# A hybrid two-block network on one core: the state space preparation's parameter chain from VectorE to GpSimd, and its within-chunk products turned round

## The chip, the core and the metric

The kernel runs on one core of a Trainium2 chip. The core has TensorE (PE in the profile; its weight loads are PEld), VectorE (DVE), ScalarE (ACT), GpSimd (POOL) and SyncE (SP, which here only issues DMAs). The time is that of one execution on the device in microseconds, a median of several runs. Beside it there is the profile of one execution, whose span runs from the first to the last instruction.

## The reference, cut to what matters

Two blocks run one after the other on a sequence of 256 tokens of 1024 channels. The first has two layers of a mixer (gated linear attention, a short convolution and latent attention side by side) and of attention over a memory. The second has two layers: a feed-forward part, a mixer, a feed-forward part. The mixer of its first layer is the state space one, the place of the change:

```python
dt = jnp.exp(log_dt)[:, None]
mag = jnp.exp(a_re * dt)
ab_re = mag * jnp.cos(a_im * dt)
ab_im = mag * jnp.sin(a_im * dt)
den = a_re * a_re + a_im * a_im
z_re = ((ab_re - 1.0) * a_re + ab_im * a_im) / den
z_im = (ab_im * a_re - (ab_re - 1.0) * a_im) / den
bb_re = z_re[..., None] * b_re - z_im[..., None] * b_im
bb_im = z_re[..., None] * b_im + z_im[..., None] * b_re
...
# x_t = ab * x_(t-1) + bb u_t (complex), by an associative scan
y = (jnp.einsum('bsgp,ghp->bsgh', x_re, c_re) - jnp.einsum('bsgp,ghp->bsgh', x_im, c_im)
     + d_skip * ug)
```

There are 64 groups of 16 channels with 64 complex states each. None of the parameters depends on the tokens.

## The kernel before, in words

Time is cut into 64 chunks of 4 tokens, and the state space layer becomes a few matrix products with tables that depend on the parameters alone. `s5_prep` makes the tables in the background of the first block and of the second block's first feed-forward part, long before `s5` reads them.

`s5_prep` first loads the parameters to 128 partitions (two groups of 64 states) x 32 columns (pairs of groups). Then follows the chain of parameters, all in 128x32 instructions: the sine and cosine (`sin_reduced`, with ScalarE), the powers 0 to 4 of a in `pw`, the powers of its phase factor up to the 128th in `E`, and z in `zr` and `zi`. A complex product is `cmul`, six instructions through `TT` (L1136). The chain stands on VectorE; one reciprocal (L1183) is in the midst of it. Its end feeds six 128x512 instructions on GpSimd that make `bb`.

Then `s5_prep_tile` runs for tiles 0 to 7, of four pairs each. A tile's steps are, in order: the load of C; X on GpSimd (tiles `pX0`, `pX1`, through `pt`); transposes of C, copied by ScalarE to `pcb` (L1249, L1250); C times powers of a on GpSimd (`pt`, then `pv`); transposes of X, copied by ScalarE (L1272) and stored; the products within a chunk, `pcb` with X, into a bank `pq`, which ScalarE copies to `pt` (L1285) and VectorE completes and spreads (L1287, L1293); the turning frame on GpSimd (`pt` and `pv` with `E`); and the last store. Stores to the stash are DMAs of GpSimd's queue.

Three things set the order. GpSimd keeps the order of the program (`InOrder`, whose helper's line L60 all its instructions carry), the foreground's few GpSimd instructions among them: `rm` and `rg` in the first block, `rf` as the first of the second block. The instructions of the other engines, and the DMAs of SyncE, are put in an order when the program is built, by a model of their times; at run time each engine keeps that order. How far the background gets is decided in `bg`, which the foreground calls after each of its steps. It gives the background a credit, a share (0.4 in the first block, 0.7 in the feed-forward part) of the counted time of the foreground's products, and each step of the background is charged with GpSimd's counted time, but 1000 at least. `InOrder` counts 2.6 ns for each column of an instruction, 0.9 for a memset and 1000 for a DMA.

Weights come in chunks through two `raw` buffers: SyncE loads (L143), ScalarE makes `hi` (L155), VectorE makes `lo` (L156), and then the buffer is free. When all steps are done, `s5_inputs` reloads some of the preparation's tiles: `bb` and two `pv` take the first tables from the stash (L1336), `prm` and `E` take other constants (L1364). These loads stand in SyncE's queue among those of the weights.

Of the kernel before, what the change touches and what calls it, by code (L numbers as in the profile page):

```python
# [14 lines left out]
AF = mybir.ActivationFunctionType  # L15
# [16 lines left out]
def ov(ap, dims):  # L32
    """The same start and partitions as ap, with other free dimensions [step, count]."""
    return bass.AP(tensor=ap.tensor, offset=ap.offset, ap=[list(ap.ap[0])] + [list(d) for d in dims])
# [14 lines left out]
class InOrder:  # L49
    """GpSimd with its instructions issued in the order of the program; counts about the ns that they take."""  # L50
# [13 lines left out]
class Products:  # L64
    """TensorE; counts about the ns that its products take."""
# [13 lines left out]
class Net:  # L79
# [13 lines left out]
    def bg(self):  # L93
        """Steps of the work in the background, in step with the products."""
        self.owed = min(self.owed + self.share * (self.PE.ns - self.at), 10000)
        self.at = self.PE.ns
        while self.owed > 0:
            g = self.G.ns
            if next(self.side, 1):
                break  # L100
            self.owed -= max(self.G.ns - g, 1000)
        self.at = self.PE.ns

    def keep_clock(self, n, p, w, x):
        """Products to a bank that nothing reads before it is written anew, in a chain of small steps: TensorE's clock
        would be halved after 3.4 us with little to do."""
        for _ in range(n):
            self.PE.matmul(p[:w.shape[-1]], w, x, start=True, stop=True)
# [28 lines left out]
    def chunk(self, parts, a, b, p=P, engine=None, to=None, rush=False, pieces=None, n=0):  # L137
        """parts: (dram access [p, .., ..], slice of b) that fill [p, a, b].  With pieces (the part of raw [p, n], the
        part of [p, a, b]) the parts are of raw instead."""
# [9 lines left out]
        # a large one in two steps, between which more urgent work can go  # L149
# [9 lines left out]
    def wcols(self, W, c0, n, k0=0, nk=KD, parted=False, **kw):  # L159
        """Columns c0.. of W [K, N] with nk tiles of 128 rows from tile k0."""  # L160
# [4 lines left out]
    def mm3(self, out, w, x, start, stop, **kw):  # L165
        """out += w.T @ x, w and x pairs of parts."""
# [5 lines left out]
    def projT(self, p, ws, x, nk=KD):  # L172
        """p [cols, i, tokens] over nk tiles of rows; ws: for each i (hi, lo) [p, nk, cols]; x (hi, lo) [p, nk, S]."""
# [5 lines left out]
    def proj2(self, w, x, m=P, n=2, tag="ps"):  # L179
        """[m, n, S] from n times m columns of the chunk w."""  # L180
# [4 lines left out]
    def rows(self, W, c0, n, x, tag="ps", take=None):  # L185
        """[tokens, n] = x.T @ W[:, c0:c0 + n], a bank for each token tile."""
# [13 lines left out]
    def rows2(self, W, c0, x, tag="ps"):  # L200
        """[tokens, t, 256] = x.T @ W[:, c0:c0 + 256], both token tiles in one bank."""
# [10 lines left out]
    def out_proj(self, W, xs, nc_, evac):  # L212
        """For each two output tiles evac(pair, psum [P, 2, S]) of W.T @ x, xs a list of pairs of parts, one for each
        tile of 128 rows; nc_ columns in a chunk."""
# [26 lines left out]
    def setup(self):  # L241
# [28 lines left out]
        # the gain of the heads of 96, four times over, in rows of 128  # L270
# [9 lines left out]
    def gain_rows(self, w, parts, eng):  # L280
        """Gains to rows of a tile (those of fewer than 128 entries twice, 64 apart)."""
# [16 lines left out]
    def load_gains(self, w):  # L298
        """The rows to columns."""
# [22 lines left out]
    def nat_T(self, xn, between=None):  # L322
        """xn [p, 2, D] natural; for each pair of tiles psum [P, 2, S]"""
# [10 lines left out]
    def nat_stats(self, xn, tag):  # L334
        """The token factor of a norm from natural rows."""
# [7 lines left out]
    def sumsq(self, src, n, tag="ps", weights=None):  # L343
        """[tokens, 2] sums over the n tiles of src [p, n, S] of their squares; next to them, [tokens, 4], the sums of
        the squares times weights by column [p, n]."""
# [22 lines left out]
    def rpow(self, ms, n, w, tag, p=P, eps=EPS, to=None):  # L368
        """(ms / n + eps) ** -0.5, [p, w]"""
# [5 lines left out]
    def bcast(self, cols, dst, tag="ps"):  # L375
        """[P tokens, 2] -> [P, S], the same on each partition."""
# [9 lines left out]
    def xhat(self, src, g, dst=None):  # L386
        """(hi, lo) of src [p, 8, S] times a gain by row."""
# [9 lines left out]
    def norm(self, gkey, l, tag):  # L397
        """Parts of hT * gain, the token factor as columns and as [P, S]."""
# [16 lines left out]
    def sin_reduced(self, out, a, k, phase, sign):  # L415
        """out = sign * sin(a + phase); k = (a + phase) / 2 pi, overwritten, as is a."""
# [12 lines left out]
    def mixer(self, l):  # L429
# [22 lines left out]
        # the weights in the order of their use, each loaded ahead of the work on the one before  # L452
# [3 lines left out]
        def heads_of(c0):  # L456
            """Heads of 48 columns to 64 apart."""
# [4 lines left out]
        def queries():  # L462
            """Heads of 64 + 32 columns, and once more the last 32 with their halves swapped."""
# [19 lines left out]
        # latent projections; glr, kr and kr with its halves swapped  # L483
# [36 lines left out]
        # gated linear attention: decays  # L520
# [31 lines left out]
        # latents, gained; keys and values  # L552
# [46 lines left out]
        # latent attention  # L599
# [40 lines left out]
        # gated linear attention: within and between chunks of 64  # L640
# [64 lines left out]
        # gates and the short convolution  # L705
# [60 lines left out]
        # products with the gates  # L766
# [14 lines left out]
    def mem_in(self, l):  # L781
        """Parts of mem * gain."""
# [48 lines left out]
    def cross(self, l):  # L831
# [6 lines left out]
        def mem_v(i):  # L838
            """The memory's values for two heads."""
# [63 lines left out]
        # the first two heads' part of three banks ahead of the rest  # L903
# [76 lines left out]
    def final_norm(self):  # L980
        """hT = norm_final(hT) and the parts of the next norm's input; returns that norm's token factor."""
# [7 lines left out]
        # with m and m2 the means of hT^2 and (hT gf)^2, the two norms' factors are f = (m + eps)^-1/2 and, in all,  # L989
        # f (f^2 m2 + eps)^-1/2 = (m2 + eps (m + eps))^-1/2  # L990
# [14 lines left out]
    def xhat_part(self, gkey, l, m2):  # L1005
        """Two tiles of the parts of hT * gain."""
# [3 lines left out]
    def pre_norm(self, gkey, l, tag, ready=False):  # L1010
        """First the parts of hT * gain, then the token factor."""
# [5 lines left out]
    def ffn(self, name, l, pre=None, out=None, then=None, rb=None):  # L1017
        """hT += 0.5 * swiglu(norm(hT)); rb: the token factor as [P, S], where it is known"""
# [10 lines left out]
        for m2 in range(KF // 2):  # L1029
            v = []  # L1030
            for c0 in (0, D_FF):
                with self.behind(self.parted if m2 == 0 and c0 else ()):
                    w = self.wcols(WI, c0 + m2 * 256, 256)
                # the third waits for the token factor, without which the first two don't leave their banks
# [54 lines left out]
    def residual_rows(self):  # L1089
        """hT back to [tokens, D]"""  # L1090
# [10 lines left out]
    # Time runs in 64 chunks of 4.  A pair of groups (32 channels, 2 x 64 states) is one matrix product:  # L1101
    # rows (time in chunk, channel) or (group, state).  Between chunks the complex recurrence is a real
    # scan in a frame that turns with the phase of a^4.
# [3 lines left out]
    def s5_prep(self):  # L1107
# [28 lines left out]
        TT = lambda o, a, b, op: V.tensor_tensor(o, a, b, op=op)  # L1136
# [9 lines left out]
        # powers 0..4 of a, and its phase factor's powers  # L1146
        V.memset(pw[:, 0, 0, :], 1.0)
        V.memset(pw[:, 1, 0, :], 0.0)
        TT(pw[:, 0, 1, :], v["mag"], v["cos"], MUL)
        TT(pw[:, 1, 1, :], v["mag"], v["sin"], MUL)  # L1150

        def cmul(o, a, b, s, E=TT):
            E(o[0], a[0], b[0], MUL)
            E(s[0], a[1], b[1], MUL)
            E(o[1], a[0], b[1], MUL)
            E(s[1], a[1], b[0], MUL)
            E(o[0], o[0], s[0], SUB)
            E(o[1], o[1], s[1], ADD)
# [8 lines left out]
        # u^4, u^8, .., u^128: cos, -sin, sin  # L1167
        E = self.pz.tile([P, 6, 3, H], F32, name="E", tag="E", bufs=1)
        cmul((E[:, 0, 0], E[:, 0, 2]), u2, u2, tmp)
        for k in range(6):  # L1170
            if k:
                cmul((E[:, k, 0], E[:, k, 2]), *2 * ((E[:, k - 1, 0], E[:, k - 1, 2]),), tmp)
            V.tensor_scalar(E[:, k, 1], E[:, k, 2], -1.0, None, op0=MUL)
# [5 lines left out]
        # z = (a - 1) / a_ct  # L1179
# [832 lines left out]
```

## Time and profile before

| | us |
|---|---|
| median of 3 runs | 1525.09 |
| lowest and highest run | 1522.07 to 1529.53 |
| span of the profiled execution | 1519.9 |
| TensorE, VectorE, ScalarE, GpSimd busy in it | 1437.0, 1016.3, 739.8, 322.0 |

A row of the profile names a line of the kernel, the engine, the operation, and what is written from what (buffer numbers left out), with partitions x columns. In a row of the timeline the first number is the start in us from the span's start, the second the time from the first start to the last end of the instructions merged in it, xN their number; in brackets stands the engine's idle time before it and who ended that. An fp32 product shows as two records. The granted clock is TensorE's share of its full speed.

### The profile page before, as it was taken

What the parts mean: (1) busy time and instruction counts of PE and PEld (TensorE: products, weight loads), DVE (VectorE), ACT (ScalarE), POOL (GpSimd) and SP (SyncE); (2) the same over time, 40 slices, a digit from 0 to 9 for tenths busy, and PEclk for the clock granted to TensorE, in tenths of its full rate; (3) what the DMA queues carried; (4) which work ended last, traced back from release to release, by engine and by line L of the source; (5) the groups of instructions that cost most, each with busy time, mean ns of one, the idle gap of its engine ahead of it and who ended that gap; (6) DMA issues with size and microseconds to landing.
All of it is one profiled execution on the core that took longest, in us unless ns stands there. A gap on an engine that the chain in (4) does not pass through costs nothing.

```text
span 1519.9 us, 28406 instructions
## 1 busy us (share of the span) xinstructions
PE 1437.0 (95%) x11767; PEld 1346.7 (89%) x11767; DVE 1016.3 (67%) x1768; ACT 739.8 (49%) x1248; POOL 322.0 (21%) x434
## 2 busy tenths in 40 slices
PE   8999999899998988997879999999999989999999
PEld 7888998889998978996769999899999976899987
DVE  6896756777676766539947764566775478666754
ACT  6844566544554443431244444455444367554442
POOL 2053432442546872003200000010000031000000
PEclk9998999999999999998899999999999988999999
DMA  7553644544645655564775555655555622155554
GB/s 193 155 152 102 205 150 124 167 132 150 212 146 163 212 201 191 184 220 170 209 149 180 194 187 181 198 184 172 171 194 177 212 81 92 38 175 183 189 188 144
DMA packets 239868, 255.58 MB, mean 168 GB/s; under 512 B 27664, under 2 KB 221145, under 8 KB 238844
## 3 DMA queue, kind: packets, MB, share of 16 engines
q1 hardware_dynamic: 234060, 234.71, 48.7%
q0 software_dynamic: 5392, 18.99, 4.7%
q8 instruction: 92, 1.51, 0.4%
q14 instruction: 36, 0.29, 0.1%
q10 hardware_dynamic: 288, 0.07, 0.0%
HBM read 235.66 MB, written 18.09 MB: 167 GB/s over the span
## 4 chain that ended last, share of the span: by engine, by line
PE 65%; DVE 9%; issue 9%; DMA 7%; POOL 7%; ACT 3%; SPq 0%; POOLq 0%; ACTq 0%; DVEq 0%
PE ps L72 56%; PE pb L72 4%; DMA raw<-in_ffn_w_in_dram 3%; POOL pv L60 3%; DVE lo L156 3%; PE pq L72 2%; POOL pt L60 2%; PE po L72 2%; DMA raw<-in_w_in_dram 1%; PE pb L76 1%; ACT hi L155 1%; POOL pX L60 1%; DMA stash<-pv 1%; DMA memn<-in_mem_dram 1%; DVE ra L1458 1%
## 5 line engine op out<-in xcount | busy, mean ns | idle before, releaser
L156 DVE TENSOR_TENSOR lo<-raw,hi 128x1024 fp32r<-128x1024 f32 (+4 forms) x383 | 486.2, 1285 | 153.2 <-PE ps L72 82.8
L155 ACT ACTIVATE hi<-raw 128x1024 fp32r<-128x1024 f32 (+2 forms) x395 | 407.6, 1072 | 327.3 <-DMA raw<-in_ffn_w_in_dram 119.7
L72 PE MATMUL ps<-xh,hi 128*128 128x256 f32 x1848 | 526.0, 285 | 13.2 <-ACT hi L155 11.2
L72 PE MATMUL ps<-xh,lo 128*128 128x256 f32 x1848 | 523.1, 283 | 7.7 <-DVE lo L156 7.6
L72 PE MATMUL ps<-xl,hi 128*128 128x256 f32 x1848 | 522.6, 283 | 0.4 <-DVE xl L392 0.4
L72 PEld LDWEIGHTS ps<-xh,hi 128*128 128x128 f32 x1848 | 351.2, 190 | 19.4 <-ACT hi L155 13.0
L72 PEld LDWEIGHTS ps<-xh,lo 128*128 128x128 f32 x1848 | 351.1, 190 | 11.8 <-DVE lo L156 9.8
L72 PEld LDWEIGHTS ps<-xl,hi 128*128 128x128 f32 x1848 | 351.1, 190 | 5.0 <-issue 3.2
L72 PE MATMUL ps<-gl,hi 128*128 128x256 f32 x576 | 164.3, 286 | 0.4 <-DVE gl L1479 0.4
L72 PE MATMUL ps<-gh,lo 128*128 128x256 f32 x576 | 164.4, 286 | 0.0
L72 PE MATMUL ps<-gh,hi 128*128 128x256 f32 x576 | 163.6, 286 | 0.5 <-ACT gh L1478 0.4
L72 PEld LDWEIGHTS ps<-gl,hi 128*128 128x128 f32 x576 | 111.3, 193 | 1.3 <-DVE gl L1479 0.6
L72 PEld LDWEIGHTS ps<-gh,hi 128*128 128x128 f32 x576 | 110.3, 193 | 1.5 <-ACT gh L1478 0.9
L72 PEld LDWEIGHTS ps<-gh,lo 128*128 128x128 f32 x576 | 110.6, 192 | 0.5 <-issue 0.2
L1040 DVE TENSOR_TENSOR ab<-ps,rbf 128x512 f32<-128x512 f32 x66 | 45.4, 689 | 76.2 <-PE ps L72 69.4
L72 PE MATMUL ps<-L,hi 128*128 128x256 f32 (+1 forms) x384 | 72.3, 286 | 1.5 <-DVE e L549 1.4
L237 ACT ACTIVATE gh<-e 128x512 fp32r<-128x512 f32 x44 | 27.7, 630 | 91.8 <-DVE e L1047 91.8
L72 PEld LDWEIGHTS ps<-L,hi 128*128 128x128 f32 (+1 forms) x384 | 58.1, 182 | 2.5 <-DVE e L549 1.7
L72 PE MATMUL ps<-L,lo 128*128 128x256 f32 (+1 forms) x192 | 53.9, 282 | 0.0
L1045 ACT ACTIVATE e<-ab 128x512 f32<-128x512 f32 x44 | 27.7, 630 | 37.1 <-DVE ab L1040 37.0
L60 POOL TENSOR_TENSOR rkvs<-rkvsa,mhalf 128x2 f32<-128x2 f32 x1 | 1.6, 1607 | 191.0 <-DVE rkvsa L371 191.0
L1046 DVE SCALAR_TENSOR_TENSOR e<-e,ab 128x512 f32<-128x512 f32 x44 | 32.6, 740 | 8.5 <-ACT e L1045 8.3
(578 smaller groups left out, 2455.1 us busy)
## 6 DMA issues: line engine op xcount, KB each, us to landing
raw<-in_ffn_w_in_dram SPq DMA_DIRECT2D x88, 1024.0 KB, 5.1
raw<-in_ffn_w_out_dram SPq DMA_DIRECT2D x34, 1024.0 KB, 5.1
stash<-pv POOLq DMA_DIRECT2D x24, 512.0 KB, 3.8
raw<-in_w_in_dram SPq DMA_DIRECT2D x11, 1024.0 KB, 8.6
raw<-in_ffn_w_out_dram SPq DMA_DIRECT2D x12, 768.0 KB, 4.6
raw<-in_w_out_dram SPq DMA_DIRECT2D x8, 1024.0 KB, 5.2
raw<-in_w_in_dram SPq DMA_DIRECT2D x14, 512.0 KB, 5.6
rec<-stash SPq DMA_DIRECT2D x4, 1536.0 KB, 7.2
```

The lines of the kernel that those rows point to most:

```text
L60: return self.tc.keep_in_program_order(f(out, *a, **k))
L72: return self.engine.matmul(out, w, x, **k)
L76: return self.engine.transpose(out, x, ident)
L155: self.nc.scalar.activation(dst(hi), src(raw), AF.Copy)
L156: (engine or self.nc.vector).tensor_tensor(dst(lo), src(raw), dst(hi).bitcast(F32), op=SUB)
L237: self.nc.scalar.activation(hi, src, AF.Copy)
L1040: V.tensor_tensor(v[-1], p, rb2, op=MUL)
L1045: A.activation(th, v[0], AF.Tanh, scale=0.5)
L1046: V.scalar_tensor_tensor(th, th, 1.0, v[0], op0=ADD, op1=MUL)
L1458: V.tensor_tensor(a[:, c, :], a[:, c, :], b[:, 1 - c, :], op=SUB if c else ADD)
```

## The change

In `s5_prep` the chain's products, sums, scalar steps and two memsets are issued on GpSimd. The reciprocal, the copies and the sine and cosine stay where they were. In `s5_prep_tile` the products within a chunk swap their operands: the 32 columns of C are the weights and the 128 columns of X move; four such products write to four times 32 rows of one bank. The bank then holds the transpose of what is wanted, so ScalarE copies it to the second 128 columns of a `pt` tile and TensorE turns it into a further bank of `pq`. Comments and descriptions of functions fall away too; those lines are left out here.

```diff
-        TT = lambda o, a, b, op: V.tensor_tensor(o, a, b, op=op)
+        TT = lambda o, a, b, op: G.tensor_tensor(o, a, b, op=op)
...
-        V.memset(pw[:, 0, 0, :], 1.0)
-        V.memset(pw[:, 1, 0, :], 0.0)
+        G.memset(pw[:, 0, 0, :], 1.0)
+        G.memset(pw[:, 1, 0, :], 0.0)
...
-        def cmul(o, a, b, s, E=TT):
-            E(o[0], a[0], b[0], MUL)
...
+        def cmul(o, a, b, s):
+            TT(o[0], a[0], b[0], MUL)
...
-            V.tensor_scalar(E[:, k, 1], E[:, k, 2], -1.0, None, op0=MUL)
+            G.tensor_scalar(E[:, k, 1], E[:, k, 2], -1.0, None, op0=MUL)
...
         V.reciprocal(v["dt"], v["t0"])
-        V.tensor_scalar(v["th"], pw[:, 0, 1, :], -1.0, None, op0=ADD)
+        G.tensor_scalar(v["th"], pw[:, 0, 1, :], -1.0, None, op0=ADD)
...
-        pg = self.ps("pq")[:, :P].rearrange("p (q c) -> p q c", q=4)
-        for q in range(4):
-            for c in range(2):
-                PE.matmul(pg[:, q, :], X[c][:, q * P:(q + 1) * P], cb[:, c, q].rearrange("p g h -> p (g h)"),
-                          start=c == 0, stop=c == 1)
+        pw_ = self.ps("pq")
+        for c in range(2):
+            for q in range(4):
+                PE.matmul(pw_[32 * q:32 * q + 32, :P], cb[:, c, q].rearrange("p g h -> p (g h)"), X[c][:, q * P:(q + 1) * P],
+                          start=c == 0, stop=c == 1, skip_group_check=True)
+        gt = self.pt()
+        gm, gw = gt[:, :P], gt[:, P:2 * P]
+        A.activation(gw, pw_[:, :P], AF.Copy)
+        pg = self.ps("pq")[:, :P]
+        PE.transpose(pg, gw, self.ident)
+        pg = pg.rearrange("p (q c) -> p q c", q=4)
         last = rec()
         tz = last[:, :512]
-        gm = self.pt()[:, :P]
```

## Rows read from the trace of the kernel before

**Rows 1.** The page's busy times: us, share of the span, instructions.
```profile
PE 1437.0 (95%) x11767; PEld 1346.7 (89%) x11767; DVE 1016.3 (67%) x1768; ACT 739.8 (49%) x1248; POOL 322.0 (21%) x434
```

**Rows 2.** Windows: length, busy us (count) of PE PEld DVE ACT POOL, clock, DMA share, GB/s.
```profile
80.00:100.00 20.00, 19.81 (x152) 18.15 (x153) 19.99 (x79) 9.45 (x17) 6.19 (x5) 1.00 0.36 106
...
110.00:115.00 5.00, 0.43 (x4) 0.23 (x2) 5.00 (x9) 2.12 (x3) 4.73 (x6) 0.78 0.82 262
115.00:124.00 9.00, 8.57 (x31) 6.41 (x32) 5.52 (x10) 3.58 (x6) 6.74 (x7) 0.55 0.22 63
```

**Rows 3.** Timeline of TensorE, 109 to 119 us.
```profile
115.43 1.54 PE L72 MATMUL po<-asT,mv 128*64 128x256 f32 x4 [4.99 <-ACT asT L627]
```

**Rows 4.** Waits of SyncE's queue, 60 to 130 us: us in total, times, longest.
```profile
SPq L143 <- DVE lo L156: 50.9, 6, 13.9
```

**Rows 5.** Waits of SyncE's queue, 440 to 620 us; timeline of TensorE behind them.
```profile
SPq L1336 <- POOL pt L60: 14.0, 1, 14.0
...
560.05 0.58 PE L72 MATMUL ps<-xh,hi 128*128 128x256 f32 x1 [5.38 <-ACT hi L155]
```

**Rows 6.** Instructions of L1136, first and last of twelve rows: ns min/median/max, starts.
```profile
L1136 DVE TENSOR_TENSOR prm<-prm x19: 179/184/506, 55.4 to 94.6; 128x32 f32<-128x32 f32 x19
...
L1136 DVE TENSOR_TENSOR r<-r x1: 186/186/186, 60.8 to 60.8; 128x32 f32<-128x32 f32 x1
```

**Rows 7.** Timeline of VectorE, ten instructions of the chain between the two starts.
```profile
75.13 0.19 DVE L1136 TENSOR_TENSOR pw<-pw,prm 128x32 f32<-128x32 f32 x1
...
76.14 0.18 DVE L1136 TENSOR_TENSOR pw<-pw 128x32 f32<-128x32 f32 x1
```

**Rows 8.** GpSimd: timeline at 150 us; its groups by form (busy, mean ns).
```profile
150.45 0.24 POOL L60 TENSOR_TENSOR pt<-pv,E 128x32 f32<-128x32 f32 x1
...
151.30 0.29 POOL L60 TENSOR_TENSOR pt<-pv,E 128x64 f32<-128x64 f32 x1
...
L60 POOL TENSOR_TENSOR pv<-pv,E 128x32 f32<-128x32 f32 x8 | 4.6, 579 | 0.0
```

**Rows 9.** Timeline of VectorE, two of the same instruction.
```profile
93.48 1.21 DVE L156 TENSOR_TENSOR lo<-raw,hi 128x1024 fp32r<-128x1024 f32 x1
...
97.21 2.08 DVE L156 TENSOR_TENSOR lo<-raw,hi 128x1024 fp32r<-128x1024 f32 x1
```

**Rows 10.** Timeline of VectorE, then GpSimd: power chain, reciprocal, bb.
```profile
74.52 0.19 DVE L1136 TENSOR_TENSOR pw<-prm 128x32 f32<-128x32 f32 x1
...
90.73 0.34 DVE L1183 RECIPROCAL prm<-prm 128x32 f32<-128x32 f32 x1
...
92.45 1.07 POOL L60 TENSOR_TENSOR bb<-pX,prm 128x512 f32<-128x512 f32 x1 [29.61 <-DVE prm L1136]
```

**Rows 11.** Timeline of TensorE: tile 4's products and what follows.
```profile
440.43 1.87 PE L72 MATMUL pq<-pcb,pX 128*128 128x32 f32 x16
442.13 0.49 PE L72 MATMUL ps<-L,hi 128*128 128x256 f32 x2
```

**Rows 12.** Timeline of TensorE at three places: 32-column weights, and transposes.
```profile
701.54 2.03 PE L72 MATMUL pq<-rs,pv 128*32 128x63 f32 x64 [8.43 <-DVE rs L1463]
...
455.49 0.66 PE L72 MATMUL pb<-sq,ones 128*32 128x256 f32 x8
455.94 0.64 PE L72 MATMUL pb<-sq,gf 128*32 128x256 f32 x8
...
473.21 1.04 PE L76 MATMUL pq<-ident,pX 128*128 128x128 f32 x8
```

**Rows 13.** Timeline of ScalarE ahead of tile 3's copy L1285.
```profile
373.76 2.01 ACT L155 ACTIVATE hi<-raw 128x1024 fp32r<-128x1024 f32 x2 [5.87 <-DMA raw<-in_w_out_dram]
```

**Rows 14.** Timeline of GpSimd: tile 4's frame and store, then the second block.
```profile
445.08 0.21 POOL L60 TENSOR_TENSOR pt<-pv,E 128x8 f32<-128x8 f32 x1 [9.82 <-DVE pv L1293]
...
456.76 0.60 POOL L60 DMA_DIRECT2D stash<-pv  x1 [0.30 <-POOL pv L60]
460.79 0.71 POOL L60 TENSOR_TENSOR rf<-rfb,mhalf 128x2 f32<-128x2 f32 x1 [3.43 <-DVE rfc L996]
```

More of the change, by code (lines that the diff above doesn't have):

```diff
@@ L1145, in s5_prep @@
         yield
-        V.memset(pw[:, 0, 0, :], 1.0)
-        V.memset(pw[:, 1, 0, :], 0.0)
+        G.memset(pw[:, 0, 0, :], 1.0)
+        G.memset(pw[:, 1, 0, :], 0.0)
         TT(pw[:, 0, 1, :], v["mag"], v["cos"], MUL)
         TT(pw[:, 1, 1, :], v["mag"], v["sin"], MUL)
-        def cmul(o, a, b, s, E=TT):
-            E(o[0], a[0], b[0], MUL)
[L1154 to L1158, printed above, removed]
+        def cmul(o, a, b, s):
+            TT(o[0], a[0], b[0], MUL)
+            TT(s[0], a[1], b[1], MUL)
+            TT(o[1], a[0], b[1], MUL)
+            TT(s[1], a[1], b[0], MUL)
+            TT(o[0], o[0], s[0], SUB)
+            TT(o[1], o[1], s[1], ADD)
         pwj = lambda j: (pw[:, 0, j, :], pw[:, 1, j, :])
@@ L1195, in s5_prep @@
         bb = self.pz.tile([P, 2, 512], F32, name="bb", tag="bb", bufs=1)
-        GT = lambda o, a, b, op: G.tensor_tensor(o, a, b, op=op)
         zb = [v[n][:, :, None].to_broadcast([P, H, 16]) for n in ("zr", "zi")]
@@ L1200, in s5_prep @@
         cmul([h16(bb[:, i, :]) for i in range(2)], [h16(t) for t in bn], zb,
-             [h16(s_) for s_ in sc], GT)
+             [h16(s_) for s_ in sc])
         yield
```

## The prediction

> **What bounds the kernel now.** I read the page first. TensorE is busy 95% of the span [rows 1], so a change can only help where TensorE stands still or where its own list of products becomes shorter. Both parts of the change lie in the preparation of the state space layer, which runs in the background of the first 600 us, so I then read two stretches of those.
>
> The first stretch is layer 0's mixer. The view by windows shows VectorE busy 19.99 of 20 us between 80 and 100 us and 5.00 of 5 us between 110 and 115 us, while TensorE has only 4 products in those last 5 us and its granted clock is 0.55 in the 9 us behind them [rows 2]. [...] There are two raw buffers, a buffer is free when VectorE has made lo of it, and ScalarE's next conversion stands in order in front of asT. So here VectorE sets the pace of the weights, and with it the pace of all.
>
> The second stretch is the head of the second block, 460 to 600 us. There GpSimd runs the tiles 5, 6 and 7 of the preparation nearly without a pause, and SyncE's queue waits 14.0 us (L1336) for the tile pt that GpSimd frees; the weight loads behind it in the same queue are late, and TensorE stands 5.38 us [rows 5]. GpSimd is little used over the span, but in this stretch its last tile sets when weights come.
>
> **The change, part by part.** *The chain leaves VectorE.* Twelve rows of L1136, from 19 instructions to 1 in each, add up to 77 products and sums of 128x32 [rows 6]; seven scalar steps and two memsets go with them. In the dense stretch ten of these instructions fill 75.13 to 76.14 us [rows 7], 0.10 us each, so VectorE gets back 84 x 0.10 = 8.4 us, nearly all between 55 and 95 us, where it has no slack. What that is worth is bounded by what TensorE loses: in the 14 us from 110 to 124 it made 35 products; at the rate of the window 80 to 100 (152 in 20 us, 0.13 us each) they take 4.6 us, so at most 9.4 us can come back [rows 2]. The lower bound is nothing, if something else arrives as late.
>
> *What GpSimd pays.* The nearest rows are its own 128x32 steps of the frame: three of them from 150.45 to 151.30 us, 0.28 us each, where VectorE leaves it alone; and a mean of 0.58 us for the eight of the dearest of these groups over the whole preparation [rows 8]. The dear ones stand beside VectorE instructions with two SBUF inputs, and the slowing is mutual: the same lo takes 1.21 us nearly alone and 2.08 us beside GpSimd's work [rows 9]. From the first step after the cosine (74.52 us) to the reciprocal (90.73 us), which stays on VectorE [rows 10], there are 73 moved instructions: 21 to 42 us on GpSimd instead of 16.2. With 0.43 us, half way, 31 us: the reciprocal's input is then 15 us later than now, and bb, which began at 92.45 us [rows 10], begins near 108 us. Two things follow. First, GpSimd's large steps of bb and of tile 0 no longer fall on VectorE's fullest 20 us, which helps. Second, VectorE now waits for GpSimd at the reciprocal, and everything behind it in VectorE's order (lo, and so the weights) waits too. If that order was laid out for GpSimd's undisturbed 0.28 us, VectorE reaches the reciprocal after 21 us, when GpSimd at 0.43 us each has done 48 of 73; the other 25 take 25 x 0.28 = 7 us with VectorE standing. That eats most of the 8.4 us. If the order has the reciprocal late enough, nothing is eaten. I take the middle of the bounds 0 and 9.4: a gain of 4.7 us.
>
> [...]
>
> *The products.* Now a tile's 8 products (16 records, 128 weight columns, 32 moving) fill 440.43 to 442.13 us: 1.70 us [rows 11]. Afterwards there are again 16 records, but of 32 weight columns and 128 moving, four beside each other. Rows of this shape: 63 moving columns, 64 records in 2.03 us, 0.03 us each; 256 moving columns, 8 records from 455.49 to 455.94 us, 0.056 us each [rows 12]. That gives 0.5 to 0.9 us; 128 lies nearer the first, so 0.5. Added are one transpose, 1.04 us for eight or 0.13 us each in a row [rows 12] and some 0.3 us alone, and a copy of 128x128 on ScalarE. Net 0.9 us a tile (0.4 to 1.1). I count tiles 0 to 4, where TensorE is the bound: 4.5 us (2 to 5.5). For tiles 5 to 7 I count nothing: there TensorE comes to stand for late weights anyway. The copy is hidden by other products that fill the place before the transpose; without that cover TensorE waits for ScalarE, which in tile 3 had two conversions, 2.01 us, in front of such a copy [rows 13].
>
> *What moves in the queue of GpSimd.* GpSimd keeps the order of the program, and bg charges each background step its counted GpSimd time, but 1000 at least. Three steps of the chain, charged 1000 each now, count 26 x 83.2 + 58 = 2221, and 28 x 83.2 = 2330 twice: 3881 more. All later steps come so much later among the foreground work. Adding up charges and credits step by step, the last three steps of tile 4 (frame and store) fall behind rf, the first GpSimd instruction of the second block. They took 445.08 to 457.36 us, in time that GpSimd otherwise spends waiting for rf's input [rows 14]; so 12.3 us enter the stretch where GpSimd's last tile decides when SyncE gets on [rows 5]. The program places tile 7 one call of bg later too, 48 products x 0.13 = 6.3 us, so weights for so long are fetched before SyncE blocks. Bounds: 0 (the whole order slides along) and 12.3. I take 12.3 - 6.3 = 6 us lost. The foreground's GpSimd instruction behind the chain in layer 0, rg, I cost at nothing: fewer steps of tile 0 stand ahead of it, and TensorE has the products of mem_k meanwhile; with that cover gone it would be late by what is left of the chain's 15 us.
>
> **Sum.** -4.7 - 4.5 + 6 = -3.2 us on the profiled span of 1519.9. The median of the runs is 1525.09, 5.2 above the span; taking that along, 1525.1 - 3.2 = 1522 us.
>
> **Rivals.** *Slower: VectorE waits at the reciprocal (L1183).* For it speak GpSimd's 0.58 us rows and VectorE's lack of slack, against it that VectorE then stops disturbing GpSimd. The point is 8.4 us of waiting. At 0.58 us GpSimd has done 36 of 73 when VectorE arrives; the other 37 take 10.5 us, and the steps done beside VectorE slow it by some 0.1 us each, another 4: VectorE is 6 us later than now, and TensorE's pause and low clock grow with it, 7 us in all. 7 - 4.5 + 6 = +8.5, 1534 us. *Faster: the order fits.* The reciprocal comes late in VectorE's order and SyncE's blocking load late in its queue: -9.4 - 4.5 + 0 = -14, 1511 us. The 50.9 us of waits on lo speak for it. *GpSimd keeps VectorE's pace:* if 73 steps take no more than the present 16.2 us, 0.22 us each, no wait arises in layer 0, and only the loss behind rf stays: -9.4 - 4.5 + 6 = -7.9, 1517 us; against it, no 128x32 row is below 0.24 us. [...] *The products give nothing:* TensorE waits about 1 us for the copy in each tile: -4.7 + 0 + 6 = +1.3, 1526 us.
>
> **How the numbers follow.** Half a per cent, 7.6 us, is about what a measurement of this kernel can tell from no change; the limits are 1517.5 and 1532.7 us. My case takes the middle half of each term's bounds: 2.4 to 7.1, 2.9 to 4.6 and 3.1 to 9.2 us, so -8.6 to +3.9, 1516 to 1529 us; it has 0.42, of which 0.04 lies below the lower limit. The order that fits has 0.18, GpSimd at VectorE's pace 0.10 (0.06 below the limit), VectorE's wait 0.22, the products that give nothing 0.08 (0.03 above the upper limit, when the whole 12.3 us are lost). Faster 0.04 + 0.18 + 0.06 = 0.28, slower 0.22 + 0.03 = 0.25, same 0.47. The range of 8 in 10 takes in the middle of the two outer rivals and some us beyond: 1509 to 1536 us.
>
> **What would show it.** Right: about 84 GpSimd instructions of 128x32 between 55 and 115 us at 0.3 to 0.6 us; VectorE under 19 of 20 us there; no 5 us pause of TensorE before 115 us; the products at about 0.5 us a tile; tile 4's frame on GpSimd after rf, and SyncE's wait for pt longer than 14 us. Wrong: an idle time of VectorE before L1183 of over 8 us; TensorE waiting for the copy ahead of the new transposes; or a stretch 460 to 600 us no longer than now.

## The result, and the profile after

The changed kernel takes 1541.2 us (median of 4 runs, 1540.05 to 1541.91) beside 1523.8 us for the kernel before on the same chip: a ratio of 1.0117, 95% interval 1.0093 to 1.0141. It is slower, by 17.4 us; the forecast was 1522 and the range ended at 1536. The profiled span is 1539.3 us.

The page's busy times of the changed kernel show what was moved and no more: against [rows 1] VectorE has 86 instructions fewer and GpSimd 86 more, and TensorE and ScalarE have 8 more each, the new turnings and copies.

```profile
PE 1437.4 (93%) x11775; PEld 1343.1 (87%) x11775; DVE 1005.2 (65%) x1682; ACT 739.4 (48%) x1256; POOL 343.9 (22%) x520
```

The windows of the changed kernel (columns as in [rows 2]) show where the time went:

```profile
80.00:100.00 20.00, 6.26 (x38) 4.94 (x36) 5.30 (x10) 3.13 (x4) 18.91 (x75) 0.68 0.17 53
...
124.00:135.00 11.00, 6.26 (x45) 5.34 (x44) 8.26 (x15) 6.28 (x8) 0.00 (x0) 0.85 0.61 194
```

In the first of them TensorE was busy 19.81 us in the kernel before and now 6.26, VectorE 19.99 and now 5.30; GpSimd, with 18.91 us, does most of what is done. The granted clock is 0.68 in that window, 1.00 before. The second window holds the pause that the forecast expected to shrink; it is still there. The timeline of VectorE in the changed kernel, two instructions that follow each other, says why:

```profile
79.92 1.23 DVE L156 TENSOR_TENSOR lo<-raw,hi 128x1024 fp32r<-128x1024 f32 x1 [0.20 <-ACT hi L155]
95.10 0.35 DVE L1183 RECIPROCAL prm<-prm 128x32 f32<-128x32 f32 x1 [13.96 <-POOL prm L60]
```

VectorE comes to the reciprocal at 81.1 us and stands for 13.96 us until GpSimd has the denominator. The timeline of GpSimd over the same time:

```profile
76.71 1.39 POOL L60 TENSOR_TENSOR pw<-prm 128x32 f32<-128x32 f32 x2 [13.38 <-ACT prm L426]
78.06 0.24 POOL L60 TENSOR_TENSOR pw<-pw 128x32 f32<-128x32 f32 x1
...
80.00 1.26 POOL L60 TENSOR_TENSOR prm<-pw 128x32 f32<-128x32 f32 x1
81.21 0.46 POOL L60 TENSOR_TENSOR pw<-pw,prm 128x32 f32<-128x32 f32 x2
...
94.30 0.77 POOL L60 TENSOR_TENSOR prm<-prm 128x32 f32<-128x32 f32 x3
...
97.63 1.24 POOL L60 TENSOR_TENSOR bb<-pX,prm 128x512 f32<-128x512 f32 x1
```

Its first power comes at 76.71 us, when the cosine is there, 2.2 us later than VectorE's in [rows 10]. When VectorE arrives 4.4 us later, 12 of the 73 steps are done; the other 61 take from 81.21 to 95.07 us, 0.23 us each, while VectorE stands still. And TensorE, in its timeline, stands for VectorE, and later for asT as it did in [rows 3]:

```profile
96.69 0.90 PE L76 MATMUL pb<-ident,as 128*128 128x128 f32 x3 [13.74 <-DVE am L659]
...
133.27 1.54 PE L72 MATMUL po<-asT,mv 128*64 128x256 f32 x4 [4.74 <-ACT asT L627]
```

To follow the loss through the program I take four products that every version has, and compare their starts in the profiled executions: A, the first turning of keT in the second layer's mixer (218.53 us in the kernel before); B, that of rf (461.56); C, the first product with gh, when the preparation is done (613.11); E, that of rkvs (978.61), behind the state space layer. The changed kernel is later by 15.4 us at A, 15.4 at B, 16.7 at C and 18.8 at E. So most of it is lost in the first layer.

### The profile page after: what moved, and what is told of

Read it like the earlier page. It is cut to its first block, busy times and chain, and to the rows that moved or that the text cites. A ratio compares the mean times of both kernels' runs of the same rounds, so it can differ in the third digit from the quotient of the medians.

```text
span 1539.3 us, 28440 instructions
## 1 busy us (share of the span) xinstructions
PE 1437.4 (93%) x11775; PEld 1343.1 (87%) x11775; DVE 1005.2 (65%) x1682; ACT 739.4 (48%) x1256; POOL 343.9 (22%) x520
## 4 chain that ended last, share of the span: by engine, by line
PE 67%; issue 8%; POOL 8%; DVE 6%; DMA 3%; ACT 2%; POOLq 0%; SPq 0%; ACTq 0%; DVEq 0%
PE ps L72 57%; PE pb L72 4%; POOL pv L60 3%; PE pq L72 2%; POOL pt L60 2%; PE po L72 2%; PE pb L76 1%; DMA raw<-in_w_in_dram 1%; DVE lo L156 1%; POOL pX L60 1%; DMA stash<-pv 1%; DVE ra L1462 0%; ACT hi L155 0%; DMA raw<-in_ffn_w_in_dram 0%; DMA raw<-in_mem_wv_dram 0%
## 5 line engine op out<-in xcount | busy, mean ns | idle before, releaser
L72 PEld LDWEIGHTS ps<-gh,lo 128*128 128x128 f32 x576 | 109.8, 191 | 11.0 <-issue 10.6
L60 POOL TENSOR_TENSOR pt<-pcb,pw 128x256 f32<-128x256 f32 x32 | 31.7, 1007 | 49.0 <-ACT pcb L1249 48.0
```

The costliest lines, as they stand in the source:

```text
L60: return self.tc.keep_in_program_order(f(out, *a, **k))
L72: return self.engine.matmul(out, w, x, **k)
```

## The experiments

Lag means the start in this version less that in the kernel before, in us. The time is the median of the version's runs, the ratio that of its runs to those of the kernel before on the same chip. "Places" are those of the background's steps among the foreground, which the account in `bg` decides.

| version | A | B | C | E | time, us | ratio to before, 95% interval |
|---|---|---|---|---|---|---|
| changed kernel | +15.4 | +15.4 | +16.7 | +18.8 | 1541.2 | 1.0117 (1.0093 to 1.0141) |
| chain_only | +13.9 | +24.1 | +27.2 | +29.7 | 1551.8 | 1.0180 (1.0134 to 1.0226) |
| products_only | -0.1 | -1.4 | -6.1 | -4.5 | 1518.9 | 0.9956 (0.9943 to 0.9970) |
| products_again | -0.9 | -3.3 | -7.1 | -4.1 | 1518.3 | 0.9956 (0.9937 to 0.9975) |
| early_recip | +10.5 | +13.3 | +6.8 | +10.3 | 1534.0 | 1.0056 (1.0036 to 1.0077) |
| early_memset | +0.4 | +5.6 | +8.4 | +11.3 | 1532.6 | 1.0042 (1.0016 to 1.0067) |
| charges_only | -2.0 | +7.4 | +13.0 | +19.0 | 1537.0 | 1.0095 (1.0059 to 1.0131) |
| products_charges | -2.0 | -1.7 | +1.0 | +6.6 | 1527.1 | 1.0017 (1.0003 to 1.0032) |
| uncharged | +21.8 | +30.6 | +29.9 | +36.8 | 1555.8 | 1.0199 (1.0170 to 1.0228) |
| memset_uncharged | +12.3 | +22.8 | +18.5 | +24.3 | 1545.8 | 1.0134 (1.0111 to 1.0157) |
| uncharged_same_places | +18.9 | +16.2 | +12.8 | +15.0 | 1539.6 | 1.0101 (1.0075 to 1.0127) |
| memset_same_places | +1.3 | -0.8 | -6.9 | -1.9 | 1524.2 | 0.9996 (0.9979 to 1.0013) |
| split | +4.2 | +10.6 | +5.2 | +13.0 | 1529.7 | 1.0039 (1.0015 to 1.0063) |
| split_memset_uncharged | -4.1 | -3.9 | -9.1 | -3.5 | 1516.2 | 0.9936 (0.9914 to 0.9958) |
| split_again | -5.0 | -7.7 | -15.1 | -11.4 | 1513.1 | 0.9934 (0.9915 to 0.9953) |

A lag compares two single executions, and the kernel before has only one. `products_again` is `products_only` once more, and `split_again` is `split_memset_uncharged`: the lags of the first pair differ by 0.4 to 1.9 us, those of the second by 0.9 us at A, 3.8 at B, 6.0 at C and 7.9 at E. Differences of a few us from B on are therefore hints; the ratios decide.

**The two halves, each alone.** `chain_only` is the changed kernel with the old products put back:

```diff
-        pw_ = self.ps("pq")
...
-        PE.transpose(pg, gw, self.ident)
...
+        for q in range(4):
+            for c in range(2):
+                PE.matmul(pg[:, q, :], X[c][:, q * P:(q + 1) * P], cb[:, c, q].rearrange("p g h -> p (g h)"),
+                          start=c == 0, stop=c == 1)
```

`products_only` is the kernel before with the new products; against the changed kernel it has all of the chain, bb's products aside, back on VectorE:

```diff
-        TT = lambda o, a, b, op: G.tensor_tensor(o, a, b, op=op)
+        TT = lambda o, a, b, op: V.tensor_tensor(o, a, b, op=op)
```

> The chain on GpSimd, but the within-chunk products as in the kernel before. Theory A (VectorE's wait at the reciprocal is the whole loss, and the new products give back some 3 us afterwards, as the lag of TensorE falls from 18.3 us at 124 us to 15.4 us at 680 us): 1523.8 + 18.3 + 3 = 1545 us at most, 1540 at least if the end of the state space stage does not lose its 3 us as well; VectorE's idle time before L1183 stays at 13 to 14 us. Theory B (the new products' waits for ScalarE's copy are a good part of the loss): 1532 to 1537 us.

> The kernel before with the new products alone; the chain stays on VectorE. Theory A: 1519 to 1523 us, some 3 us less than before; TensorE has no new wait before 120 us. Theory B: 1527 to 1532 us, with waits of 1.5 to 4 us for the copy in several tiles.

The products alone make the kernel faster by 0.44%, as theory A had it and theory B did not. The chain alone costs 1.8%, 7 us more than theory A allowed: its lag at A is near that of the changed kernel, but another 13.3 us come between A and C. So theory B falls, and A does not explain all.

The gain of the products comes late: next to nothing at A, and 4.7 of the 6.1 us between B and C. There, in the waits of SyncE's queue of `products_only` from 440 to 620 us, the wait for `pt` is 11.6 us instead of 14.0 [rows 5]:

```profile
SPq L1341 <- POOL pt L60: 11.6, 1, 11.6
```

and in the timeline of TensorE the pause for `hi` behind it is 2.36 us instead of 5.38 [rows 5] (4.08 us in `products_again`), though it now waits for the new copy as well:

```profile
523.52 0.33 PE L76 MATMUL pq<-ident,pt 128*128 128x128 f32 x1 [1.74 <-ACT pt L1283]
...
554.85 0.38 PE L72 MATMUL ps<-xh,hi 128*128 128x256 f32 x1 [2.36 <-ACT hi L155]
```

**The reciprocal's input early.**

```diff
         TT(v["th"], v["aim"], v["dt"], MUL)
+        V.tensor_tensor(v["t0"], v["are"], v["are"], op=MUL)
+        V.tensor_tensor(v["t1"], v["aim"], v["aim"], op=MUL)
+        V.tensor_tensor(v["t0"], v["t0"], v["t1"], op=ADD)
+        V.reciprocal(v["dt"], v["t0"])
...
-        TT(v["t0"], v["are"], v["are"], MUL)
...
-        V.reciprocal(v["dt"], v["t0"])
```

> The changed kernel with the denominator's three steps and the reciprocal on VectorE, right behind th, ahead of the chain, so that VectorE does not wait for GpSimd there; the chain stays on GpSimd. Theory A: the 14 us of idle time are gone, the lag at 124 us falls from 18.3 us to between -5 and +2 us, and the time is 1516 to 1526 us. Theory C (GpSimd's slower chain itself makes something late: bb and tile 0, and by the charges tile 4's last steps behind the first GpSimd instruction of the second block): 1530 us or more, the lag then growing between 430 and 600 us.

VectorE's 14 us are gone, 0.6% of the time with them, but the lag at A is still 10.5 us. That is not theory A; the time is where theory C had it, but the lag does not grow behind the first layer as C said. The timelines of ScalarE, VectorE and TensorE in `early_recip` show the same wait at the next place:

```profile
108.72 0.22 ACT L1248 ACTIVATE pcb<-pq 64x64 f32<-64x64 f32 x1 [17.37 <-POOL pcb L60]
...
110.43 0.17 DVE L615 RECIPROCAL ast<-ast 128x2 f32<-128x2 f32 x1 [16.48 <-ACT as L614]
...
112.29 0.58 PE L72 MATMUL ps<-xh,lo 128*128 128x256 f32 x1 [12.20 <-DVE lo L156]
```

ScalarE has tile 0's copy to `pcb` next in its order. That copy needs a memset of `pcb`, 0.31 us of work at 108.38 us, which stands in GpSimd's queue behind the whole chain and behind bb. Behind the copy on ScalarE stand foreground instructions, and VectorE and TensorE wait for those.

**That memset moved ahead of the chain as well.**

```diff
+        cb0 = self.pt("pcb", 1).rearrange("p (a q g h) -> p a q g h", a=4, q=4, g=2)
+        G.memset(cb0[:, 0:2], 0.0)
         G.memset(pw[:, 0, 0, :], 1.0)
```

> As early_recip, and tile 0's memset of pcb stands ahead of the chain in GpSimd's queue instead of behind the chain and bb. Theory A2 (it was never the reciprocal as such: whatever stands in another engine's order behind GpSimd's chain holds that engine; with the reciprocal out of the way ScalarE waited 17.4 us for this memset, and VectorE 16.5 us for ScalarE): both waits are gone, no stall of TensorE over 6 us between 80 and 130 us, the lag behind the kernel before at 124 us between -4 and +4 us, the time 1514 to 1524 us. Theory C (the chain on GpSimd costs by itself, through what GpSimd does later): the next instruction that needs GpSimd waits in its turn, lag over 8 us at 124 us, the time 1530 us or more.

Now the lag at A is 0.4 us. The loss in the first layer is shown to be waits at two places in other engines' orders that stand behind GpSimd's chain. But the time is still 0.4% above before, 8 us above the most that theory A2 allowed; the lag grows by 8.0 us between A and C.

**The places alone.** The kernel before, with nothing moved, only counted:

```diff
-        TT = lambda o, a, b, op: V.tensor_tensor(o, a, b, op=op)
+        def TT(o, a, b, op):
+            G.ns += 2.6 * width(o)
+            return V.tensor_tensor(o, a, b, op=op)
```

> The kernel before, its chain on VectorE and its products as they were, but every step of the chain counted in GpSimd's account as in the changed kernel, so that later background steps come as much later among the foreground work. If the prediction's term of +6 us for tile 4's last steps behind rf is right: 1528 to 1533 us, and the stretch 460 to 600 us of before is some 6 us longer. Theory A and A2 (that shift costs nothing): within 0.4% of before, 1518 to 1529 us.

> The new products and the shift by the charges, the chain on VectorE: all of the change but the engine of the chain. If the parts add up: products_only at -6.8 us and charges_only at +12.4 us at 702 us give +5 to +7 us there, 1528 to 1533 us, and the engine of the chain alone then makes up the rest of the changed kernel's loss. If the shift costs only beside the old products: 1516 to 1522 us.

`charges_only` has the old products, `products_charges` the new ones. Counting alone costs 0.95% beside the old products, more than the forecast term (the medians, 1537.0 and 1525.7 us, are 0.74% apart): 9.4 us between A and B and 5.6 between B and C. In the timeline of GpSimd in `charges_only`, tile 4's last store now stands behind rf, 12 us into the second block; in [rows 14] it stood ahead of it:

```profile
468.89 0.69 POOL L60 TENSOR_TENSOR rf<-rfc,mhalf 128x2 f32<-128x2 f32 x1
...
480.87 0.62 POOL L60 DMA_DIRECT2D stash<-pv  x1 [0.30 <-POOL pv L60]
```

Beside the new products the same counting costs 0.6% (1.0017 beside 0.9956 of `products_only`), and from A to C `products_charges` loses 3.0 us where `products_only` gains 6.0. So the places cost. That they cost less beside the new products isn't clear of the noise.

In the traces GpSimd does the same steps in the same order in `products_charges` and in the changed kernel, apart from the chain. Between these two lies the chain's engine alone: 1.0%.

**The places of before, the chain on GpSimd.** Two kernels in which the chain's steps are issued without being counted:

```diff
-        TT = lambda o, a, b, op: G.tensor_tensor(o, a, b, op=op)
+        keep = self.tc.keep_in_program_order
+        TT = lambda o, a, b, op: keep(nc.gpsimd.tensor_tensor(o, a, b, op=op))
```

> The changed kernel with the chain's steps not counted in GpSimd's account, so that each background step is charged as in the kernel before and later steps stand where they stood. Theory A: the wait at L1183 stays, 1537 to 1543 us, within 0.3% of the changed kernel. Theory C (the charges' shift costs): some 6 us less than the changed kernel, 1535 us or below.

> As early_memset (no wait behind GpSimd's chain in layer 0), and the chain's steps not counted in GpSimd's account, so that all later background steps stand where they stood in the kernel before. If the loss of the changed kernel is the sum of the waits behind the chain and of the shift by the charges, both are gone, and what is left is the new products and VectorE's freed time: the lag behind the kernel before is -3 to -8 us at 613 us, the time 1513 to 1520 us, as products_only or a little below. If GpSimd's later chain makes tile 0 and what follows late all the same (theory C): 1526 us or more, with stalls of TensorE for GpSimd's rg or for pv between 120 and 450 us as in uncharged.

`uncharged` came out slower than either theory had it, and `memset_uncharged` is no 1513 to 1520 us but has the stalls that theory C named. The reason is in the edit: in the changed kernel bb's six products go through the same `TT`, so they fell out of the account too. Every later step came 6 x 2.6 x 512 - 1000 = 6987 counted ns earlier than in the kernel before. What that did is seen in the timeline of TensorE in `memset_uncharged`: it now stands for tile 0's X, and in the second layer for `on`, because GpSimd's foreground step rg stands behind a tile's frame and store:

```profile
120.30 1.11 PE L76 MATMUL pq<-ident,pX 128*128 128x128 f32 x4 [9.01 <-POOL pX L60]
...
381.54 0.69 PE L76 MATMUL pb<-ident,on 128*128 128x128 f32 x2 [6.33 <-DVE on L703]
```

The timeline of GpSimd in the same kernel has that order:

```profile
378.60 0.60 POOL L60 DMA_DIRECT2D stash<-pv  x1 [0.30 <-POOL pv L60]
379.22 1.67 POOL L60 TENSOR_TENSOR rg<-rga,mhalf 128x8 f32<-128x8 f32 x1
```

With bb counted again (`self.G.ns += 6 * 2.6 * 512` ahead of it) the order of GpSimd's other steps is that of `products_only`, but for the memset where it was moved:

> As memset_uncharged, but with bb's six steps (7987 counted ns) charged again, which go by the same function as the chain and had fallen out of the account there too; now every background step stands exactly where it stands in the kernel before. If the loss was the sum of the waits behind the chain and of shifted places: both are gone, lag at the first keT transpose (218 us) between -2 and +4 us, at the end of the feed-forward part's first half (613 us) -6 to 0 us, 1516 to 1522 us. If a chain on GpSimd, 8 us later with bb than on VectorE, is too late for the places of before: TensorE waits for pX near 120 us, lag over 6 us at 218 us, 1526 us or more.

> As uncharged, with bb's steps charged again: the changed kernel with every background step where it stands in the kernel before, the waits at the reciprocal and behind it as they are. By the sum of waits and places: lag +14 to +17 us at 218 us as in the changed kernel, then some 6 us given back by the new products up to 613 us, 1530 to 1536 us. If places of before are too early for a chain that ends late: lag above 20 us at 613 us, 1543 us or more.

From A to C these two gain 8.3 and 6.2 us, as the products alone do. `memset_same_places`, free of the waits and at the old places, takes what the kernel before takes; `uncharged_same_places`, with the waits, takes 1% more. Between them lie only the edits that end the waits: 1539.6 - 1524.2 = 15 us, and 17.6 us at A. The expected 1530 to 1536 us for the latter were too low, since its lag at A is 18.9 us and not 14 to 17. The expected 1516 to 1522 us for the former were too low as well: it has the new products, and yet it is 0.4% slower than `products_only`, and the two intervals do not meet. So at the same places and without the waits the chain on GpSimd still costs some 6 us. The lags at C are the same; where the 6 us are lost isn't shown.

**Part of the chain.** Only E and r4, 44 steps on which no other engine waits, go to GpSimd, with scratch of their own; products as in the changed kernel. The second version also has tile 0's memset first and doesn't count the 44 steps (bb is counted):

```diff
+        tmg = u1
-        cmul((E[:, 0, 0], E[:, 0, 2]), u2, u2, tmp)
+        cmul((E[:, 0, 0], E[:, 0, 2]), u2, u2, tmg, GT)
```

> The new products, and only E and r4 (44 steps) on GpSimd; the powers, the denominator and z stay on VectorE, so that the reciprocal needs nothing of GpSimd. By theory A (VectorE's wait alone) no wait of VectorE for GpSimd, 1515 to 1520 us. By theory A2 GpSimd has bb and tile 0's memset of pcb behind its 44 steps (44 x 0.25 = 11 us) and ScalarE may wait for that memset some 5 us: 1518 to 1528 us.

> As split (only E and r4 on GpSimd), with tile 0's memset of pcb ahead of them and these 44 steps not counted. By the same sum: no wait behind GpSimd in layer 0, no shift; 1512 to 1520 us. Theory C: 1524 us or more.

> products_only once more, beside the others on one chip: 1517 to 1522 us by every theory; it says which of these versions is the fastest.

> split_memset_uncharged once more, with more rounds: 1514 to 1518 us, 0.4 to 0.8% below the kernel before, by every theory.

`split` has no wait at the reciprocal, but ScalarE waits 11.1 us for the memset of `pcb`, and the lag at A is 4.2 us; its time is just above theory A2's 1528 us. Without that wait and at the old places it has the lowest ratios, 0.64% and 0.66% below the kernel before in its two comparisons; their intervals overlap those of the products alone (0.44%), so that the time does not show it to be faster than those. Its first layer is where VectorE's time is seen to be worth something. The timeline of TensorE has the pause for asT, 4.99 us in [rows 3], at 2.21 in `split_memset_uncharged`, and at 1.88 in `split_again`:

```profile
114.26 0.86 PE L72 MATMUL po<-asT,mv 128*64 128x256 f32 x4 [2.21 <-ACT asT L627]
...
112.53 0.86 PE L72 MATMUL po<-asT,mv 128*64 128x256 f32 x4 [1.88 <-ACT asT L627]
```

## Why the prediction was wrong, step by step

**The failed step** is in "What GpSimd pays": "VectorE reaches the reciprocal after 21 us, when GpSimd at 0.43 us each has done 48 of 73". It reached it after 4.4 us, when 12 were done. I took the order of VectorE to be laid out for GpSimd's time from the chain's first step. It was not: nothing but two lo and a few short instructions stood in it between the cosine and the reciprocal. Foreground work that the kernel before does ahead of its reciprocal at 90.73 us, L725, L659 and L720, stands behind the reciprocal in the changed kernel. The timelines of VectorE show its first instruction, in the kernel before and in the changed one:

```profile
82.34 0.68 DVE L725 TENSOR_TENSOR e<-ps,rb 128x512 f32<-128x512 f32 x1
...
95.37 0.63 DVE L725 TENSOR_TENSOR e<-ps,rb 128x512 f32<-128x512 f32 x1
```

The first power also came 2.2 us later than before, and for a reason that I had not looked at: the two steps of the chain ahead of the sine and cosine now stand behind the foreground's rm in GpSimd's order, and rm waits for VectorE. They ran at 62.75 us and not at 55.38, and the sine and cosine behind them came later. The timelines of VectorE before and of GpSimd in the changed kernel:

```profile
55.38 0.28 DVE L1136 TENSOR_TENSOR prm<-prm 128x32 f32<-128x32 f32 x2
...
62.09 0.69 POOL L60 TENSOR_TENSOR rm<-rma,mhalf 128x2 f32<-128x2 f32 x1 [23.10 <-DVE rma L371]
62.75 0.46 POOL L60 TENSOR_TENSOR prm<-prm 128x32 f32<-128x32 f32 x2
```

Why the model put the reciprocal so early in VectorE's order no run shows. So the estimated 7 us of waiting were 13.96, and the term of -4.7 us became +15.4 at A. The text named this itself as what would show it wrong: an idle time of over 8 us before L1183. The range left it out, because the rival was priced with a wait of 10.5 us after the same 21.

**GpSimd's price was too high, not too low.** I took 0.43 us a step; the 73 steps took 18.4 us, 0.25 each, and bb began at 97.63 us, not 108. The first 12, beside VectorE's work, took 4.5 us, 0.38 each, and the 61 after VectorE stood 0.23 each. At VectorE's own pace, 16.2 us, the wait would still have been some 16.2 - 4.4 = 11.8 us, by this estimate: the rival in which GpSimd keeps pace and no wait arises had the wrong premise too. Another point against that rival, that no such row is below 0.24 us, took a step's length for its pace: the lengths overlap (the steps at 81.63 and 81.83 us of the changed kernel last 0.24 us each and start 0.20 us apart). Of the eight steps behind the mean of 0.58 us four are short, 0.24 to 0.25 us; of the four dear ones three were caught beside a lo (0.69, 1.22 and 1.31 us), the fourth, 0.44 us, beside L392. One of them in the timelines of GpSimd and VectorE of the kernel before:

```profile
381.04 1.31 POOL L60 TENSOR_TENSOR pv<-pv,E 128x32 f32<-128x32 f32 x1
...
381.03 2.40 DVE L156 TENSOR_TENSOR lo<-raw,hi 128x1024 fp32r<-128x1024 f32 x2
```

The step at 80.00 us of the changed kernel is alike (1.26 us beside a lo of 1.23). No run shows the 0.1 us by which, in the slower rival, each such step was to slow VectorE: the two lo beside the chain, at 76.55 and 79.92 us, took 1.22 and 1.23 us, against 1.21 nearly alone in [rows 9]. While VectorE stands still, GpSimd has 0.23 us between steps, where VectorE has 0.10 in [rows 7]. Half of my 0.43 us came from rows beside a busy VectorE.

**What stands behind the reciprocal.** I named what waits for VectorE, but not the other places at which an engine's order needs GpSimd. ScalarE's copy to `pcb` was one: freed of the first wait, the kernel waited 17.4 us there. The exponential of `mag`, behind rm and the chain's first step, is another: ScalarE waits 0.59 us for it in the changed kernel (63.03 us), and 1.88 us in `memset_same_places` (65.12 us), where the two larger waits are gone. No run takes this one away.

**VectorE's freed time.** In `memset_same_places` 83 instructions are gone from VectorE and nothing waits at the reciprocal or the memset, but it is slower than `products_only` (0.9996 and 0.9956 of before). The pause for asT that the freed time was to shorten is still there in its timeline of TensorE, 5.57 us instead of the 5.18 of `products_only` (116.18 us):

```profile
120.96 1.54 PE L72 MATMUL po<-asT,mv 128*64 128x256 f32 x4 [5.57 <-DVE sg L635]
```

So nothing of the 9.4 us is seen with the whole chain, and my lower bound, nothing, was too high: some 6 us are lost that I had no term for. With the 44 steps that nobody waits for, the pause is 3 us shorter than in `products_only` and the lag at A 3 to 5 us less: there VectorE's time does count.

**The products.** The price of a tile was right. In the timeline of TensorE in the changed kernel the 16 records of a tile take 0.58 us to the next product instead of 1.70 [rows 11], and the turning 0.03 us where it stands among other products (up to 0.26 in other tiles). That is up to 1.1 us less a tile, and 0.4 to 1.1 were forecast:

```profile
402.53 0.64 PE L72 MATMUL pq<-pX,pcb 128*32 128x128 f32 x16
403.11 0.51 PE L72 MATMUL ps<-eb,hi 128*128 128x256 f32 x2
...
403.69 0.27 PE L76 MATMUL pq<-ident,pt 128*128 128x128 f32 x1
403.72 0.37 PE L72 MATMUL ps<-ei,hi 128*128 128x256 f32 x1
```

The place was wrong. I counted 4.5 us for tiles 0 to 4 and nothing for 5 to 7, because TensorE stands there for late weights. The runs show the reverse, 1.4 to 3.3 us up to B and 3.8 to 4.7 from B to C. That a shorter tile lets GpSimd's last tile, and so SyncE's load, end sooner is what the shorter wait for `pt` suggests; no run isolates it.

**The queue of GpSimd.** That tile 4's last steps fall behind rf was right, and so was the sign that SyncE's wait for `pt` grows, from 14.0 us to 15.2. The timeline of GpSimd in the changed kernel, then the waits of SyncE's queue from 440 to 620 us:

```profile
476.92 0.69 POOL L60 TENSOR_TENSOR rf<-rfc,mhalf 128x2 f32<-128x2 f32 x1
...
488.89 0.63 POOL L60 DMA_DIRECT2D stash<-pv  x1 [0.30 <-POOL pv L60]
```

```profile
SPq L1340 <- POOL pt L60: 15.2, 1, 15.2
```

The size behind rf fits too: 5.6 us in `charges_only`, 6 forecast, though lags of single executions can't show it to the us. I costed only this one meeting of background and foreground; the other 9.4 us in that run come between A and B. "Nearly without a pause" was too strong: between 460 and 600 us of the kernel before GpSimd is busy for 95.02 us of 140. In the changed kernel little of it is left: it is 4 us behind `uncharged_same_places` at C, and in time 1541.2 beside 1539.6 us, too close to tell apart. A shift in the other direction cost no less: against `memset_same_places` the 7 counted us of `memset_uncharged` cost 1.4% of the time. rg, costed at nothing in the first layer, cost nothing there: GpSimd had waited 33.07 us for its input (154.92 us).

**In sum** the changed kernel's 1.17% can be laid out in two ways, by ratios to the kernel before. At the old places: products -0.44 (`products_only`), the chain on GpSimd +1.45 (`uncharged_same_places`), places +0.16, too little to tell from nothing. Of the 1.45, 1.05 go with the two waits (`memset_same_places`), some 15 us; 0.40, some 6 us, stay and aren't explained. At the new places: products -0.44, places +0.61 (`products_charges`), the chain +1.00, of which 0.75 go with the waits (`early_memset`). Each row ends at 1.17 because its terms are differences between neighbours, so the sums prove nothing. The waits are the largest term in both, in the second by no more than the noise.

**Left open.** Every version loses 1.6 to 7.8 us between C and E against the kernel before. Part of that may be the one execution of the kernel before. Another part is a wait of TensorE in the state space layer that the profile gives to "issue": in the timelines of the kernel before, then of the changed one,

```profile
768.41 0.58 PE L72 MATMUL po<-gh,hi 128*128 128x256 f32 x1 [7.91 <-issue]
```

```profile
786.82 0.58 PE L72 MATMUL ps<-gh,lo 128*128 128x256 f32 x1 [10.36 <-issue]
```

The wait is there in every version, 7.91 us in the kernel before and 8.11 to 10.74 in the others. No run was made to change it, and what holds it isn't shown. Nor is it shown where the chain on GpSimd costs what is left without the waits: `early_memset`, with the same order of GpSimd's steps as `products_charges`, loses 8.0 us between A and C and not 3.0, but the lags can't tell these apart.

## What to carry to other kernels

Moving work to an idle engine is not free when other engines keep an order that was fixed earlier: look for each instruction elsewhere that needs anything in the moved engine's queue behind the moved work (here a reciprocal, then a 0.3 us memset), and ask how much other work each engine has in its order ahead of that place, counted from when the chain's own input comes; the chain's length does not tell. Move what nobody waits for soon. And where an account of estimated times paces background work, changing what is counted moves every later step, which cost 0.95% in one direction here and 1.4% in the other.

## What the runs showed of the hardware

In the changed kernel 61 steps of 128x32 on GpSimd took 0.23 us each while VectorE stood still (81.21 to 95.07 us). A step that started during VectorE's lo (128x1024, 79.92 us) took 1.26 us (80.00 us) and ended 0.1 us behind the lo; the steps behind it took 0.23 to 0.31.

Eight products of 32 weight columns and 128 moving ones, four side by side in one bank, took 0.58 us for their 16 records (402.53 us in the changed kernel), against 1.70 us for 16 records with 128 weight columns and 32 moving [rows 11]: with the same count, shape and placing together were worth a factor of 2.9. No run parts the two.
